# One pair of the third SwiGLU's down projection, seven products or eight

## The chip, the cores and the metric

The kernel runs on one core of a Trainium2 chip. A core has TensorE (PE in the profile; its weight loads are shown apart as PEld), VectorE (DVE), ScalarE (ACT), GpSimd (POOL) and SyncE (SP), which issues most DMA transfers. The metric is the time of one execution in device microseconds (us). The kernel before takes 942.07 us, the median of 3 runs (941.84 to 942.65).

## What is computed

A trunk of two layers over 256 tokens of width 1024, all in float32. Each layer adds half a SwiGLU, a mixer (attention), and half a SwiGLU again:

```python
def swiglu(h, w_gate, w_up, w_down):
    return (jax.nn.silu(h @ w_gate) * (h @ w_up)) @ w_down
...
    for layer in range(DEPTH):
        i = layer // 2
        h = rms_norm(x, ffn1_norm[layer])
        x = x + 0.5 * swiglu(h, ffn1_w_gate[layer], ffn1_w_up[layer], ffn1_w_down[layer])
        h = rms_norm(x, mix_norm[layer])
...
        h = rms_norm(x, ffn2_norm[layer])
        x = x + 0.5 * swiglu(h, ffn2_w_gate[layer], ffn2_w_up[layer], ffn2_w_down[layer])
    return rms_norm(x, final_norm)
```

The hidden width of a SwiGLU (D_FF) is 2816. So w_down is 2816 x 1024, or 22 blocks of 128 rows.

## The kernel before

**Stages.** There are six stages, counted from 0: SwiGLU, even mixer, SwiGLU, SwiGLU, odd mixer, SwiGLU. The third SwiGLU is stage 3; the odd mixer, stage 4, follows it. The 256 tokens are two tiles of 128 (tt 0 and 1). A stage's input is transposed on TensorE and split (`prepare`, L521), so that every matmul has it as the stationary operand, and the weights stream as the moving operand, 512 columns at a time.

**A product is three matmuls.** Float32 is reached with two parts of a value each, hi and lo. ScalarE writes hi (L479), VectorE writes lo = value - hi (L482), and a product of a left block and a piece of weights of 128 x 512 is hi x hi, hi x lo and lo x hi (`mm`, L462; the three matmuls are L471 to L473). Weights come from memory in transfers of 1 MB (`load`, L369) into one of 3 "raw" buffers, are split in two or four steps, and a raw buffer takes the next transfer when the lo of its last split is written. The split parts go into 7 buffers (hi/lo, "wp") or, where sums of weights are split, into 3 others (shi/slo, "sum").

**The order is written by hand.** Each engine works through its instructions in the order in which the program issues them. A planner decides where a weight split is issued among the products: every product is a tick (L274), a tick adds `rate` to a credit, and when the credit covers the next split and one of its buffers is free by the planner's count (`room`, L287), the hi is issued now and the lo one tick later (`supply`, L417; `low`, L438). Other work runs as small tasks that wait a written number of ticks.

**The down projection.** Its 22 row blocks are 11 pairs: pair n has blocks 2n and 2n + 1, one transfer. The list DOWN (L36) gives the order of the pairs in each stage and the form of each: `p` is a plain pair, `s` one with seven products. A plain pair takes 2 blocks x 2 token tiles x 2 halves of the 1024 columns = 8 products. A pair with seven products (`seven`, L908) takes the 2 x 2 blocks (two token tiles and two row blocks on the left, two row blocks and two column halves on the right) in Strassen's manner:

```python
            temp("1", "pj", gT[0][f + 1], b11)
...
            self.mm(Y[0][0], gT[0][f], b21, False, False)
            self.mm(Y[0][1], d4, b22, False, False)
            temp("7", "tp", d3, t7)
            temp("5", "s", d1, t5)
            self.mm(Y[1][0], gT[1][f], t8, False, False)
            temp("6", "tp", d2, t6)
```

Three go straight into the sums Y; the four called temp add up in banks of their own over all the pairs with seven products. For this the weights need four sums of 128 x 512 (t5 to t8), made on VectorE beside the splits (`strassen`, L392, L395: a "two" of 1024 columns and two steps of 512), and the left side needs four combinations of its four blocks (`quarters`, L696, and `sums_of`, L711: copies on ScalarE into the one "quarters" buffer, three steps on VectorE, then hi and lo into tiles named k and the number of the pair's first block, as k12h and k12l of pair 6). After the last pair with seven products ScalarE copies half of product 1, and `combine` (L935) adds the temps to x in eight VectorE steps spread over eight ticks. At the same place the planner's rate, 1.32 in this part (DOWN_RATE), is set to 0.34 and its credit to 3 (ENDS, L48). The last two pairs of the list are "held": their products are ordered by token tile and column half, so that each sum Y ends early, is added to x on VectorE (L614), and the next stage's transposes (L527) can begin.

**The gate and up projections of a stage** use seven products too, in two of their chunks in stage 3 (`seven_gates`, L756). The left combinations for these, four tiles called K, lie in buffers of tiles that come into use later: after two of g, in the k tiles of the two highest blocks among the pairs with seven products (the list `places` in `x_sums`, L727).

Of the kernel before, what the change touches and what calls it, by code (L numbers as in the profile page):

```python
# [35 lines left out]
DOWN = {  # L36
    0: "p0 p1 p2 s3 p4 s5 p6 s7 p8 p10 p9",
    2: "p0 p2 p1 p3 s5 p4 s7 p10 s8 p6 p9",
    3: "p0 p2 s5 s3 p4 s8 p10 s6 p1 p9 p7",
    5: "p3 p0 s2 s5 p4 s1 p9 s7 s8 p6 p10",  # L40
}

# [1525 lines left out]
```

## Time and profile before

| | |
|---|---|
| median of the runs (3) | 942.07 us (941.84 to 942.65) |
| the profiled execution | 941.97 us |
| its span, first to last instruction | 940.1 us |
| granted TensorE clock, mean | 0.998 |
| stage 3, down: first product to the next stage's first | 576.87 to 637.45 us of the span |
| DMA, mean over the span | 195 GB/s |

Times in the views are us from the span's start. A timeline row is: start, duration, engine, line, operation, written tile <- read tiles, shape, and in brackets the time for which the engine stood idle before it with what released it. Matmuls overlap, so the distance from one start to the next tells the pace. The brackets give the writer that came last, by the profile.

### The profile page before, as it was taken

Reading aid. Unit: us, or ns where it says so; the run is one execution under the profiler, and the core shown is the slowest. Engines: PE = TensorE matmul, PEld = TensorE weight load, DVE = VectorE, ACT = ScalarE, POOL = GpSimd, SP = SyncE. Lnnn points to the kernel's source line nnn. Section 1 sums busy time; section 2 is a strip of 40 time slices with the busy share of each in tenths; the row PEclk is TensorE's granted clock in tenths of the full one; section 3 lists DMA queues with packets and bytes.
Section 4 is the critical chain, followed back from the end, with each engine's and each line's share of the span. In section 5 each row is a group of like instructions: output and inputs, shape, how many; then the busy total and the mean of one; then the engine's idle time right before and its main releaser. Section 6 shows DMA issues by size and latency. Waiting matters only on the chain.

```text
span 940.1 us, 12389 instructions
## 1 busy us (share of the span) xinstructions
PE 921.0 (98%) x4399; PEld 752.3 (80%) x4399; DVE 783.1 (83%) x1212; ACT 677.5 (72%) x1091; POOL 92.6 (10%) x152
## 2 busy tenths in 40 slices
PE   9999999999999999999999999999999999999997
PEld 6887888877778787888888878778878788878886
DVE  6799778778869989888978897989767687987897
ACT  7778975477787778875657778657877577769753
POOL 1300000064410000000100000008030000000001
PEclk9999999999999999999999999999999999999999
DMA  8858875554326577767466777575534358487851
GB/s 302 286 158 250 250 235 193 181 151 108 100 91 201 203 233 230 237 211 250 153 183 223 199 235 227 204 250 172 169 102 137 132 180 245 139 254 228 218 224 45
DMA packets 129344, 183.16 MB, mean 195 GB/s; under 512 B 50689, under 2 KB 63745, under 8 KB 129281
## 3 DMA queue, kind: packets, MB, share of 16 engines
q1 hardware_dynamic: 128704, 181.58, 61.2%
q8 instruction: 34, 0.56, 0.2%
q10 hardware_dynamic: 576, 0.79, 0.2%
q14 instruction: 30, 0.24, 0.1%
HBM read 169.76 MB, written 1.05 MB: 182 GB/s over the span
## 4 chain that ended last, share of the span: by engine, by line
PE 65%; DVE 17%; ACT 10%; DMA 4%; issue 3%; POOL 0%; SPq 0%; POOLq 0%; ACTq 0%; DVEq 0%
PE pj L471 9%; PE pj L472 9%; PE pj L473 9%; PE s L472 9%; PE s L473 9%; PE s L471 9%; DVE lo L482 7%; ACT hi L479 3%; DMA glu<-turned 2%; ACT turned L560 2%; DVE raw L395 2%; PE o L1042 2%; ACT shi L479 2%; PE tp L1119 1%; PE o L472 1%
## 5 line engine op out<-in xcount | busy, mean ns | idle before, releaser
L482 DVE TENSOR_TENSOR lo<-raw,hi 128x1024 fp32r<-128x1024 f32 (+1 forms) x372 | 376.3, 1031 | 78.0 <-ACT hi L479 76.5
L479 ACT ACTIVATE hi<-raw 128x1024 fp32r<-128x1024 f32 (+1 forms) x372 | 318.6, 889 | 49.3 <-PE s L473 15.1
L471 PE MATMUL pj<-hi,th 128*128 128x512 f32 x367 | 146.7, 400 | 0.9 <-ACT glu L766 0.9
L471 PE MATMUL s<-hi,th 128*128 128x512 f32 x373 | 146.2, 392 | 0.4 <-ACT hi L479 0.4
L472 PE MATMUL pj<-lo,th 128*128 128x512 f32 x367 | 143.9, 392 | 2.6 <-DVE lo L482 2.3
L472 PE MATMUL s<-lo,th 128*128 128x512 f32 x373 | 145.5, 390 | 1.0 <-DVE lo L482 1.0
L473 PE MATMUL s<-hi,tl 128*128 128x512 f32 x373 | 145.3, 390 | 0.0
L473 PE MATMUL pj<-hi,tl 128*128 128x512 f32 x367 | 143.2, 390 | 0.0
L472 PEld LDWEIGHTS pj<-lo,th 128*128 128x128 f32 x367 | 69.0, 188 | 17.9 <-DVE lo L482 5.4
L472 PEld LDWEIGHTS s<-lo,th 128*128 128x128 f32 x373 | 70.1, 188 | 16.3 <-DVE lo L482 2.1
L471 PEld LDWEIGHTS s<-hi,th 128*128 128x128 f32 x373 | 70.0, 188 | 14.8 <-ACT hi L479 0.6
L473 PEld LDWEIGHTS s<-hi,tl 128*128 128x128 f32 x373 | 70.0, 188 | 14.6
L471 PEld LDWEIGHTS pj<-hi,th 128*128 128x128 f32 x367 | 69.0, 188 | 15.4 <-ACT glu L766 1.3
L473 PEld LDWEIGHTS pj<-hi,tl 128*128 128x128 f32 x367 | 68.9, 188 | 14.6
L491 POOL TENSOR_TENSOR rstd<-var,mhalf 128x1 f32<-128x1 f32 (+2 forms) x16 | 17.1, 1069 | 593.7 <-ACT th L512 314.7
L560 ACT COPY turned<-glu 128x1024 uint16<-128x1024 uint16 (+1 forms) x48 | 60.1, 1253 | 9.7 <-DMA glu<-turned 9.7
L479 ACT ACTIVATE shi<-raw 128x1024 fp32r<-128x1024 f32 x30 | 31.7, 1058 | 42.9 <-DVE raw L395 26.1
L556 ACT COPY turned<-glu 128x1024 uint16<-128x1024 uint16 (+1 forms) x48 | 46.4, 966 | 21.7 <-DVE glu L794 15.7
L471 PE MATMUL s<-hi,g_h 128*128 128x512 f32 (+1 forms) x131 | 51.3, 392 | 0.0
L473 PE MATMUL s<-hi,g_l 128*128 128x512 f32 (+1 forms) x131 | 50.8, 388 | 0.0
L472 PE MATMUL s<-lo,g_h 128*128 128x512 f32 (+1 forms) x131 | 50.8, 388 | 0.0
L482 DVE TENSOR_TENSOR slo<-raw,shi 128x1024 fp32r<-128x1024 f32 x30 | 36.7, 1223 | 10.8 <-ACT shi L479 10.4
(482 smaller groups left out, 1671.1 us busy)
## 6 DMA issues: line engine op xcount, KB each, us to landing
raw<-in_ffn_w_down SPq DMA_DIRECT2D x44, 1024.0 KB, 5.1
raw<-in_ffn_w_up SPq DMA_DIRECT2D x28, 1024.0 KB, 5.3
raw<-in_ffn_w_gate SPq DMA_DIRECT2D x26, 1024.0 KB, 5.2
raw<-in_ffn_w_gate SPq DMA_DIRECT2D x35, 512.0 KB, 4.1
raw<-in_ffn_w_up SPq DMA_DIRECT2D x32, 512.0 KB, 5.0
raw<-in_odd_w_qkv SPq DMA_DIRECT2D x12, 1024.0 KB, 5.1
raw<-in_even_w_in SPq DMA_DIRECT2D x4, 1024.0 KB, 5.2
raw<-in_even_w_out SPq DMA_DIRECT2D x8, 512.0 KB, 5.8
```

Source lines behind the costliest of these rows:

```text
L395: add = lambda o, x, y: self.nc.vector.tensor_tensor(o, x, y, op=ALU.add)
L471: mm(ps, h, wh, start=first, stop=False)
L472: mm(ps, h, wl, start=False, stop=False)
L473: mm(ps, l, wh, start=False, stop=last)
L479: self.nc.scalar.activation(hi, src, AF.Copy)
L482: self.nc.vector.tensor_tensor(lo, src, hi.bitcast(F32), op=ALU.subtract)
L491: nc.gpsimd.tensor_tensor(r[:, :n], v[:, :n], self.mhalf[:, :n], op=ALU.pow)
L556: self.nc.scalar.copy(planes.rearrange("p (h c) -> p h c", h=2), back.rearrange("p (c h) -> p h c", h=2))
L560: self.nc.scalar.copy(planes.rearrange("p (c h) -> p h c", h=2), back.rearrange("p (h c) -> p h c", h=2))
L1042: self.nc.tensor.matmul(O[64 * s : 64 * s + 64, i * P : i * P + P], v(b0 + i, s, kc), pT[s][:, i, kc, :], start=(kc == 0), stop=(kc == 1),)
L1119: nc.tensor.transpose(tb[:, o : o + P], p[:, i, kc * P : kc * P + P], self.ident)
```

## The change

The letter of one pair in the list of stage 3: pair 6, eighth of eleven, becomes plain.

```diff
 DOWN = {
     0: "p0 p1 p2 s3 p4 s5 p6 s7 p8 p10 p9",
     2: "p0 p2 p1 p3 s5 p4 s7 p10 s8 p6 p9",
-    3: "p0 p2 s5 s3 p4 s8 p10 s6 p1 p9 p7",
+    3: "p0 p2 s5 s3 p4 s8 p10 p6 p1 p9 p7",
     5: "p3 p0 s2 s5 p4 s1 p9 s7 s8 p6 p10",
 }
```

Pair 6 then takes eight products where it took seven. Its sums of weights (L395) and the combinations of blocks 12 and 13 (L701 to L715, k12h and k12l) are not made; its weights are split as two splits of two pieces, in wp buffers. Pairs 5, 3 and 8 keep the seven products. The last of them is now pair 8, sixth in the list, so the half copy of product 1, `combine` and the setting of the planner to ENDS follow pair 8 instead of pair 6, two pairs earlier:

```python
        order = [i for i, (kind, _) in enumerate(down) if kind == "strassen"]
        for i, (kind, pair) in enumerate(down[:-HELD]):
            if kind == "strassen":
                seven(pair, i == order[0], i == order[-1])
                if i == order[-1]:
                    self.start(combine())
                    self.rate, self.due = ENDS[self.now.n]
                continue
```

The two highest blocks among the pairs with seven products are 16 and 10 where they were 16 and 12, so the fourth of the K tiles lies in k10h and k10l where it lay in k12h and k12l.

## The prediction

> **What bounds the kernel now.** I read the busy totals first, then the windows over the stage that changes, then TensorE's timeline in it, and last the chain of waits behind each gap.
>
> ```profile
> PE 921.0 (98%) x4399; PEld 752.3 (80%) x4399; DVE 783.1 (83%) x1212; ACT 677.5 (72%) x1091; POOL 92.6 (10%) x152
> ```
>
> ```profile
> 576.87:589.11 12.24, 12.24 (x55) 10.14 (x54) 9.98 (x13) 9.85 (x15) 0.00 (x0) 1.00 0.55 142
> 589.11:598.05 8.94, 8.52 (x37) 6.60 (x36) 8.87 (x14) 7.14 (x12) 0.00 (x0) 1.00 0.36 122
> 598.05:608.25 10.20, 10.20 (x46) 8.45 (x45) 10.16 (x12) 6.42 (x7) 0.00 (x0) 1.00 0.65 235
> 608.25:618.45 10.20, 10.20 (x46) 8.45 (x45) 10.09 (x11) 5.92 (x6) 0.00 (x0) 1.00 0.69 261
> 618.45:630.70 12.25, 12.25 (x55) 9.95 (x53) 10.77 (x16) 5.83 (x9) 0.00 (x0) 1.00 0.78 276
> 630.70:637.45 6.75, 5.23 (x27) 4.27 (x27) 5.23 (x13) 4.36 (x14) 0.20 (x1) 1.00 0.42 150
> ```
>
> A window's row gives its length, then the busy time of PE, PEld, DVE, ACT and POOL, the granted clock (1.00 throughout) and DMA. The third SwiGLU's down projection is 576.87 to 637.45. TensorE is busy in all but two windows; in the second and the last it loses time. VectorE is full from 589 to 618 (8.87 of 8.94, 10.16 of 10.20, 10.09 of 10.20). So TensorE sets the end, and here VectorE sets TensorE's two gaps:
>
> ```profile
> 576.87 0.39 PE L471 MATMUL o<-hi,g_h 128*128 128x512 f32 x1
> ...
> 596.79 0.50 PE L472 MATMUL s<-slo,g_h 128*128 128x512 f32 x1 [0.42 <-DVE slo L482]
> ...
> 598.05 0.39 PE L471 MATMUL o<-hi,g_h 128*128 128x512 f32 x1
> ...
> 630.47 0.39 PE L473 MATMUL s<-hi,g_l 128*128 128x512 f32 x1
> 632.37 0.66 PE L527 MATMUL tp<-mats,x 128*128 128x128 f32 x4 [1.52 <-DVE x L614]
> ...
> 637.45 0.40 PE L471 MATMUL pj<-hi,th 128*128 128x512 f32 x1
> ```
>
> The price of a matmul is its distance to the next, not its 0.39 us. From 598.05 to 630.47 lie 143 steps (48 products of three, less one): 32.42 / 143 = 0.2267 us. A product is 0.680 us.
> From 576.87 to 598.05 lie 30 products, 20.40 us at that pace, and they took 21.18: **0.78 us** lost in the first gap (0.42 shown idle, the rest slower starts round it). At the end the transposes could start at 630.47 + 0.23 = 630.70 and start at 632.37: **1.67 us** lost in the second.
>
> **The change part by part.** (1) TensorE. Pair 6 takes four piece rows by two token tiles: 8 products where the seven-product form takes 7. One product more, 3 x 0.2267 = **+0.68 us**, on the bounding engine, hidden by nothing.
>
> (2) VectorE, in the down stage. What goes is in these rows, start to start:
>
> ```profile
> 605.73 2.96 DVE L482 TENSOR_TENSOR lo<-raw,hi 128x1024 fp32r<-128x1024 f32 x3
> 608.60 1.22 DVE L395 TENSOR_TENSOR two<-raw 128x1024 f32<-128x1024 f32 x1
> 609.74 1.22 DVE L482 TENSOR_TENSOR lo<-raw,hi 128x1024 fp32r<-128x1024 f32 x1
> 610.87 0.69 DVE L395 TENSOR_TENSOR raw<-two,raw 128x512 f32<-128x512 f32 x1
> 611.59 0.69 DVE L395 TENSOR_TENSOR raw<-raw 128x512 f32<-128x512 f32 x1
> 612.20 1.22 DVE L482 TENSOR_TENSOR slo<-two,shi 128x1024 fp32r<-128x1024 f32 x1
> 613.49 1.23 DVE L482 TENSOR_TENSOR slo<-raw,shi 128x1024 fp32r<-128x1024 f32 x1
> 614.63 4.63 DVE L482 TENSOR_TENSOR lo<-raw,hi 128x1024 fp32r<-128x1024 f32 x4
> ```
>
> The last of the three at 605.73 (2.87 less two full lows of 1.14, 0.6) and all until 614.63 is pair 6: 0.6 + 6.0 = 6.6 us. A plain pair is two lows, 2.3 us. VectorE sheds 4.3 us, ScalarE the matching highs. The load is the same 1,024 KB at the same place of SP's queue.
>
> (3) The left factors of pair 6 (blocks 12 and 13) lose their combinations:
>
> ```profile
> 574.55 0.28 DVE L714 TENSOR_TENSOR quarters<-quarters 128x128 f32<-128x128 f32 x1
> 574.87 0.29 DVE L715 TENSOR_TENSOR quarters<-quarters 128x128 f32<-128x128 f32 x1
> ...
> 581.50 0.68 DVE L482 TENSOR_TENSOR k12l<-quarters,k12h 128x512 fp32r<-128x512 f32 x1
> 583.62 0.48 DVE L677 SCALAR_TENSOR_TENSOR glu<-s,rstd,silu 128x256 f32<-128x256 f32 x1 [1.43 <-ACT silu L672]
> ```
>
> ```profile
> 576.55 1.05 ACT L479 ACTIVATE hi<-raw 128x1024 fp32r<-128x1024 f32 x1
> 577.50 0.62 ACT L479 ACTIVATE k12h<-quarters 128x512 fp32r<-128x512 f32 x1
> ...
> 582.28 0.42 ACT L701 ACTIVATE quarters<-turned 128x256 f32<-128x256 f32 x1 [2.39 <-DVE k12l L482]
> ```
>
> VectorE sheds about 1.2 us here (0.3 and 0.3, and 0.6 of k12l), ScalarE k12h. More than that: there is one "quarters" buffer, and pair 8's ScalarE copy waits 2.39 us for k12l to release pair 6's; behind it stand the silu for which VectorE idles 1.43 us, and the highs of the first sums. Nothing of pair 6 is left to wait for. I walked both queues from 574 with the rows' durations: VectorE's two lows of pair 5's sums end at 584.1, the last low of pair 3's sums, for which TensorE waits at 596.79, at about 593.6 instead of 596.7. TensorE wants it at product 28, 595.9. So the **0.78 us** of the first gap go, with 2.3 us in hand. What is late next there is that low itself: its buffer is released by pair 5's third and fourth products (about 591.4), so it can hardly come sooner.
>
> (4) The last seven-product pair is now pair 8. ScalarE's half copy of product one, the eight combining steps and the switch to ENDS (0.34 per product, credit 3) move two pairs forward, past p10 and the old pair 6.
>
> ```profile
> raw<-in_ffn_w_down SPq DMA_DIRECT2D x44, 1024.0 KB, 5.1
> ```
>
> ```profile
> 614.75 0.37 SPq L379 DMA_DIRECT2D raw<-in_ffn_w_down  x1
> ```
>
> ```profile
> 619.58 2.01 ACT L479 ACTIVATE hi<-raw 128x1024 fp32r<-128x1024 f32 x2 [2.33 <-DMA raw<-in_ffn_w_down]
> ```
>
> ```profile
> 620.67 3.58 DVE L482 TENSOR_TENSOR lo<-raw,hi 128x1024 fp32r<-128x1024 f32 x4 [1.41 <-ACT hi L479]
> 624.17 0.68 DVE L941 SCALAR_TENSOR_TENSOR x<-pj,x 128x512 f32<-128x512 f32 x1
> ...
> 630.42 1.29 DVE L482 TENSOR_TENSOR lo<-raw,hi 128x512 fp32r<-128x512 f32 x2
> 631.63 0.69 DVE L614 SCALAR_TENSOR_TENSOR x<-o,x 128x512 f32<-128x512 f32 x1
> ```
>
> Before, the add to x that the next stage's transposes wait for (631.63) stands in VectorE's queue behind the combining steps and odd lows (624.17 to 631.63), four lows before them, and a 1.41 us wait for highs that wait 2.33 us for pair 7's load: that one was issued at 614.75, when the second sums' low of the old pair 6 released its buffer. Now that buffer is released by p6's second low, at about 607. I counted the planner's credits product by product (call the first of down 0). Pair 8's sevens end after product 44. Highs then come only as a released buffer allows: pair 9's second at product 49, pair 7's at 53 and 57, the first odd pieces at 61, 62, 65, 67, 70 and 73. All of pair 6, pair 1 and half of pair 9 are made before that. With releases at TensorE's pace and loads landing 5.1 us after issue, VectorE is through with combining near 618, with pair 7's second low near 620.4 (TensorE wants it at product 72, 576.87 + 72 x 0.680 = 625.8), and free for the add to x when its sum ends, about 627.0 to 627.7. The transposes stand before product 79, at 630.6. So the **1.67 us** go too, 3 us in hand. TensorE then waits for nothing in this stage. Of the moved steps the copy stands behind pair 1's highs on ScalarE, which wait for pair 1's load; combining follows it, and behind combining stand the lows of pairs 9 and 7, the ones with 5 us in hand. None issues a DMA; SP's queue keeps its order with pair 7 and the first odd loads issued some 6 us earlier, and POOL has no work in these windows (0.00) to be moved past.
>
> (5) What follows. Entering the odd stage the count gives the same credit (0.02), the same five live buffers and the same order as before, one product later. So that stage is not rearranged, only moved. Its loads are issued earlier, not later.
>
> (6) The K[3] factors of the gate stages take the buffer of block 10 (pair 5) instead of block 12 (pair 6), which block 10's own factors overwrite later:
>
> ```profile
> L472 PE MATMUL tp<-slo,k12h x4: 389/389/389, 492.2 to 539.1; 128*128 128x512 f32 x4
> ```
>
> ```profile
> 552.63 0.61 ACT L479 ACTIVATE k10h<-quarters 128x512 fp32r<-128x512 f32 x1
> ```
>
> The last read is at 539.1, the overwrite at 552.63: a new wait with 13 us in hand, nothing. Were that cover gone, ScalarE would stand there, with the highs behind it. The buffers that block 12 no longer needs let the pool's last tiles sit 4 KB lower; over those the odd stage lays its attention outputs, which it makes last, so that costs nothing either.
>
> **Sum.** +0.68 - 0.78 - 1.67 = -1.77 us. The profiled execution took 941.97 us for a span of 940.1; it would take 940.20, span 938.3. The median of the runs is 0.10 above it: 942.07 - 1.77 = **940.3 us**, 0.19% less. About 0.2%, 1.9 us, is what a measurement of this kernel tells from no change, so the likeliest verdict is "within 0.2%", close to the edge.
>
> **A rule that speaks against it.** TensorE is at 98% busy and VectorE at 83%. The Trainium skill, "Perfetto Trace Analysis", section "Identifying the Most-Contended Engine", says to take the engine of highest occupancy for the bottleneck and to optimize that one first; by it this change loads the wrong engine, and the sum would be the +0.68 of step 1 instead of -1.77. The same page of the Trainium skill, section "Optimization Strategy", adds that the most contended engine can change between regimes; the windows above agree (VectorE 10.16 of 10.20 us), and that is why I do not follow the whole-span rule here.
>
> **The rivals.** *Only the product counts.* Both gaps stay: another wait on ScalarE (a transposed tile's DMA) takes the place of the quarters buffer, combining takes the place of pair 6: 942.07 + 0.68 = 942.75. Against it stand the 5.5 us that VectorE sheds; for it, that VectorE stays nearly full until 611. This is the case of the Trainium skill's rule above. *The first gap stays*, the second goes: 942.07 + 0.68 - 1.67 = 941.1. For it: the chain through DMA transposes and one quarters buffer is long, and I have walked it with medians. *The second stays*, the first goes: 942.07 + 0.68 - 0.78 = 942.0. For it: odd lows still stand ahead of the add to x.
> *Slower: starved at the held pairs.* Credit 0.34 now rules 40 products instead of 24, and the held pairs use four splits within four products (69 to 72). Pairs 9 and 7 are made one by one behind releases; a late one costs a high (0.95, from 576.55 to 577.50) and a low (1.14) in a row, 2.1 us. With two late: 940.3 + 4.2 = 944.5. It decides where pair 7's second low comes after 625.8; I have it at 620.4, so VectorE would have to be 5.4 us behind my walk. That the change does not do what it says cannot be: the counts are fixed.
>
> **How the numbers follow.** Both gaps go: 0.70 (its own range 939.8 to 940.8). The first stays: 0.09. The second stays: 0.07. Only the product counts: 0.06. Starved: 0.08. The range for 8 in 10 takes in the first three: 939.7 to 942.0. Faster begins below 940.19, 0.11 under the forecast: a bit under half of the first case lies there, 0.32. Slower, above 943.95, holds the starved case but for a mild one, 0.07. The rest, 0.61, is within.
>
> **What would show it.** Right: no PE idle by slo between 594 and 598, no ACT wait for k-low before L701 near 580, transposes of the next stage right behind their matmul, combining near 612 to 618, and the odd stage's first matmul at 635.7. Wrong: a PE wait at the held pairs; the odd stage gaining PE waits of its own, which would return what was won; a first odd matmul later than 637.

## The result and the profile after

The changed kernel takes **940.45 us** (median of 19 runs, 940.16 to 941.56), the kernel before, measured beside it, 941.98 us (19 runs). The ratio over all the runs is **0.9982**, 95% interval 0.9976 to 0.9988; of the two medians it is 0.9984. The forecast was 940.3 us and "within 0.2%". The profiled execution took 940.38 us for a span of 938.5.

The busy totals of the changed kernel:

```profile
PE 921.4 (98%) x4402; PEld 753.3 (80%) x4402; DVE 777.6 (83%) x1203; ACT 675.8 (72%) x1086; POOL 92.7 (10%) x152
```

TensorE has three matmuls more and the same share of the span; the totals don't show what happened. The windows over the stage do (columns as before: length, busy time of PE, PEld, DVE, ACT and POOL with counts, granted clock, DMA share, GB/s; cut at places that answer to those of before):

```profile
576.72:588.96 12.24, 12.24 (x56) 10.14 (x55) 11.29 (x16) 11.40 (x18) 0.00 (x0) 1.00 0.76 220
588.96:597.90 8.94, 8.94 (x41) 7.42 (x40) 8.91 (x11) 5.50 (x8) 0.00 (x0) 1.00 0.36 110
597.90:608.10 10.20, 10.20 (x47) 8.45 (x46) 9.69 (x11) 6.19 (x7) 0.00 (x0) 1.00 0.68 256
608.10:618.30 10.20, 10.20 (x47) 8.45 (x46) 9.04 (x12) 6.35 (x7) 0.00 (x0) 1.00 0.72 273
618.30:630.55 12.25, 12.25 (x57) 10.10 (x55) 8.01 (x12) 3.46 (x6) 0.00 (x0) 1.00 0.75 258
630.55:635.48 4.93, 4.93 (x27) 4.11 (x26) 3.03 (x9) 4.37 (x14) 0.22 (x1) 1.00 0.00 2
sum 58.76, PE 58.76 PEld 48.66 DVE 49.97 ACT 37.28 POOL 0.22; mean PE 9.79 PEld 8.11 DVE 8.33 ACT 6.21 POOL 0.04
```

TensorE is busy for the whole of every window: both gaps are gone. VectorE and ScalarE do in the first window what they could not do before (11.29 of 12.24 us where it was 9.98; 11.40 where it was 9.85): the wait for the quarters buffer is not there. From 608 on VectorE has room, which it did not have before (9.04 of 10.20 against 10.09).

The stage, from its first product to the next stage's first, takes 635.48 - 576.72 = **58.76 us**, where it took 637.45 - 576.87 = 60.58: **-1.82 us**, with -1.77 forecast. From here on this stage time is the measure: it depends least on what lies elsewhere in the execution.

ScalarE's timeline, where the 2.39 us wait stood:

```profile
578.14 1.38 ACT L560 COPY turned<-glu 128x1024 uint16<-128x1024 uint16 x1 [0.81 <-DMA glu<-turned]
579.55 0.42 ACT L701 ACTIVATE quarters<-turned 128x256 f32<-128x256 f32 x1
```

The copy into quarters waits for nothing. What ends last there now is the transposing DMA ahead of it, 0.81 us. VectorE's timeline at the places that the prediction named:

```profile
583.02 1.22 DVE L482 TENSOR_TENSOR slo<-raw,shi 128x1024 fp32r<-128x1024 f32 x1
...
592.79 1.22 DVE L482 TENSOR_TENSOR slo<-raw,shi 128x1024 fp32r<-128x1024 f32 x1
...
612.70 0.68 DVE L941 SCALAR_TENSOR_TENSOR x<-pj,x 128x512 f32<-128x512 f32 x1
...
617.68 1.28 DVE L939 TENSOR_TENSOR x<-x,glu 128x512 f32<-128x512 f32 x2
618.88 4.76 DVE L482 TENSOR_TENSOR lo<-raw,hi 128x1024 fp32r<-128x1024 f32 x6
...
626.55 0.69 DVE L614 SCALAR_TENSOR_TENSOR x<-o,x 128x512 f32<-128x512 f32 x1 [0.76 <-PE o L473]
629.27 0.69 DVE L614 SCALAR_TENSOR_TENSOR x<-pj,x 128x512 f32<-128x512 f32 x1 [2.03 <-PE pj L473]
```

The low for which TensorE had waited ends at about 594.0 (592.79 + 1.22) where it ended near 596.7. Combining runs from 612.70 to 618.96. The adds to x now wait for TensorE's sums, 0.76 and 2.03 us; before, TensorE waited 1.52 us for one of them. TensorE's timeline has no bracket from 576.72 to the odd stage:

```profile
595.75 0.39 PE L471 MATMUL s<-shi,g_h 128*128 128x512 f32 x1
595.98 0.39 PE L472 MATMUL s<-slo,g_h 128*128 128x512 f32 x1
...
630.21 0.39 PE L473 MATMUL s<-hi,g_l 128*128 128x512 f32 x1
630.44 0.60 PE L527 MATMUL tp<-mats,x 128*128 128x128 f32 x4
...
635.48 0.39 PE L471 MATMUL pj<-hi,th 128*128 128x512 f32 x1
```

The matmul at 595.98 is the one that stood behind the first gap. It starts 0.23 us after the matmul before it, where that step took 0.81 us (595.98 to 596.79 before). Up to the transposes one matmul follows the next at 0.227 us, and the transposes start 0.23 us behind the matmul before them.

### The profile page after: what moved, and what is told of

Its sections match the earlier page's. It is cut to its first block, busy times and chain, and to the rows that moved or that the text cites. A ratio compares the mean times of both kernels' runs of the same rounds, so it can differ in the third digit from the quotient of the medians.

```text
span 938.5 us, 12381 instructions
## 1 busy us (share of the span) xinstructions
PE 921.4 (98%) x4402; PEld 753.3 (80%) x4402; DVE 777.6 (83%) x1203; ACT 675.8 (72%) x1086; POOL 92.7 (10%) x152
## 4 chain that ended last, share of the span: by engine, by line
PE 76%; DVE 11%; ACT 8%; issue 3%; DMA 2%; POOL 0%; SPq 0%; POOLq 0%; ACTq 0%; DVEq 0%
PE s L472 10%; PE s L473 10%; PE s L471 10%; PE pj L471 10%; PE pj L472 10%; PE pj L473 10%; DVE lo L482 5%; ACT hi L479 3%; PE o L473 2%; PE o L472 2%; PE o L471 2%; PE o L1042 2%; ACT turned L560 2%; DMA glu<-turned 1%; PE tp L1119 1%
```

## The experiments

The result agrees with the steps, but several things changed at once: the quarters buffer, VectorE's work, the place of combining. Each was changed alone. (A "seven" is a pair with seven products; a "gap" is one of TensorE's two, behind product 28 and ahead of the transposes.) In what follows "stage" is the time from the first product of stage 3's down projection to the odd stage's first; 60.58 us before, 58.76 after. In one repetition of the changed kernel, `after_again`, it was 58.77, so it repeats to some hundredths. Each stage time is of one profiled execution. "Measured" gives the ratio to the kernel before with its 95% interval of about 0.0009 to each side, 0.9 us; so the ratios do not tell most of these kernels apart.

**1. The quarters wait alone.** The kernel before, all four sevens kept; block 12's high is issued four ticks sooner, and its low stands one tick closer behind it, so five ticks sooner in all:

```diff
-            yield SUMS_WAIT[0]
+            early = self.now.n == 3 and f == 12
+            yield 4 if early else SUMS_WAIT[0]
...
-            yield SUMS_WAIT[1]
+            yield 1 if early else SUMS_WAIT[1]
```

> Four pairs keep the seven products, as before; only the hi and lo of pair 6's left combinations are issued five products sooner, so that the quarters buffer is free for pair 8. Stage time is from the first down product to the odd stage's first (60.58 us before, 58.76 after the change). Theory, the first gap is the wait for the quarters buffer and the second is VectorE's lag carried on: the gap at product 28 closes (0.78 us), VectorE runs some 2 us ahead from there and the second gap closes wholly or mostly: stage 58.1 to 58.9 us, 939.5 to 940.4 us in all, with no product added. Rival, the amount of work that pair 6 puts on VectorE makes both gaps: stage 60.3 to 60.6 us, about 942. Between them, only the first gap closes: 59.8 us, 941.2.

Measured: ratio 0.9986 (0.9977 to 0.9996), stage **58.90 us**. ScalarE's row in this kernel, and TensorE's one row with a wait:

```profile
580.56 0.42 ACT L701 ACTIVATE quarters<-turned 128x256 f32<-128x256 f32 x1
```

```profile
631.39 0.44 PE L527 MATMUL tp<-mats,x 128*128 128x128 f32 x2 [0.61 <-DVE x L614]
```

The wait at L701 is gone and with it the whole first gap; of the second 0.77 us are left (0.61 shown idle). So these two waits (the numbers behind the two `yield`s) are worth 60.58 - 58.90 = 1.68 us in the stage without a product more. The work of VectorE and ScalarE is the same as before; only its order differs. The quarters buffer was behind the first gap and behind more than half of the second. In the whole less of it arrived: the medians are 942.52 and 941.73 us, 0.79 apart. Run 9 shows where 0.9 us went.

**2. Combining late.** The changed kernel with the combining and the switch to ENDS put back behind pair 6:

```diff
-                if i == order[-1]:
-                    self.start(combine())
-                    self.rate, self.due = ENDS[self.now.n]
+                if i == order[-1] and self.now.n != 3:
+                    close()
...
+            if self.now.n == 3 and pair == 6:
+                close()
```

> The changed kernel with combining and the switch of the planner's rate put back behind pair 6, where they were before. Theory, the second gap closed because VectorE sheds work and a raw buffer is released sooner, not because combining moved: stage 58.8 us, 940.4 us in all, the transposes not waiting. Rival, it closed because combining moved two pairs forward: the wait of the transposes for the add to x returns, up to 1.67 us, stage up to 60.4 us, 942.1.

Measured: 0.9983 (0.9974 to 0.9992), stage **58.75 us**, no gap. Where combining stands made no difference here: VectorE's add to x ends at 629.18 us, and TensorE comes to the transposes at 631.93, 2.75 us later.

**3. The combinations of blocks 12 and 13 kept**, though nothing reads them:

```diff
+        if self.now.n == 3:
+            paired[12] = []
```

> The changed kernel, but the left combinations of pair 6 are still made (and not used), so the quarters buffer is held for them as before and the K tiles lie where they lay. Theory, the quarters buffer alone makes the first gap: ScalarE's wait of about 2.4 us for k12's lo returns, and with it a wait of TensorE at product 28 of 0.4 us idle, 0.7 to 0.8 us with the slower starts; the second gap stays closed: stage 59.5 us, 941.2 us in all. Rival, the first gap closed because VectorE has less of anything queued: stage 58.8, 940.4.

Measured: 0.9983 (0.9974 to 0.9992), stage **59.64 us**. ScalarE's row, and TensorE's:

```profile
582.98 0.42 ACT L703 ACTIVATE quarters<-turned 128x256 f32<-128x256 f32 x1 [2.40 <-DVE k12l L482]
```

```profile
597.47 0.50 PE L472 MATMUL s<-slo,g_h 128*128 128x512 f32 x1 [0.42 <-DVE slo L482]
```

The wait is back with 2.40 us, and the first gap with the 0.42 us idle of before (0.87 in all, where it was 0.78: the steps round it are a little slower). The second stays closed: by then VectorE has made up the delay. Together with run 1 this settles the first gap.

**4. Two sevens.** The changed kernel with pair 8 plain too, the last two K tiles in k16 and k12 as in the kernel before, and the switch to ENDS left behind pair 8 (those lines are not shown); combining moves up behind pair 3:

```diff
-    3: "p0 p2 s5 s3 p4 s8 p10 p6 p1 p9 p7",
+    3: "p0 p2 s5 s3 p4 p8 p10 p6 p1 p9 p7",
...
+            tops = [16, 12] if self.now.n == 3 else sorted(paired, reverse=True)
```

> The changed kernel with pair 8 plain as well (two pairs with seven products are left; the planner's rate is still switched behind pair 8). No gap is left to close, so this prices one product by itself. Theory: plus 0.68 us, stage 59.44 us, 941.1 us in all. Rival, relieving VectorE goes on paying: 940.4 or less. If combining still earlier or pair 8's two wp splits collide with the buffers, a wait shows in the stage and it is over 941.5.

Measured: 0.9982 (0.9973 to 0.9991), stage **59.42 us**, no gap: 0.66 more than with three sevens. That is the price of a product, 0.68 by the prediction. With no gap left to close, relieving VectorE once more returns nothing.

**5. VectorE's work put back.** The changed kernel; behind the two lows of pair 6 stand four sums of 128x1024 on a spare tile, which nothing reads:

```diff
+        def spare():
+            for view in views:
+                two = self.t([P, 2, 512], "two")
+                self.nc.vector.tensor_tensor(two, view, view, op=ALU.add)
+
+        return [Split(view, [2], view is views[-1], then=spare) for view in views]
```

> The changed kernel with four VectorE sums of 128x1024 (1.14 us each, 4.6 us in all) on a spare tile put back at pair 6's place, behind its two lows; they are not used. So VectorE has the work that the change took away, TensorE keeps its extra product, and combining stays two pairs forward. Theory (the gaps went by the quarters buffer and by combining early; VectorE had 8.8 us idle in the stage after the change): still no gap, stage 58.8 us, within 0.2. Rival (the gaps went because VectorE has less to do): the second gap is back, stage 60 to 60.4.

Measured: 0.9981 (0.9972 to 0.9990), stage **58.76 us**. The stage in one window:

```profile
578.56:637.32 58.76, 58.76 (x264) 48.64 (x263) 54.30 (x71) 37.18 (x58) 0.22 (x1) 1.00 0.63 208
```

VectorE is busy for 54.30 us of it, nearly the 55.10 of before, and TensorE waits for nothing. The sums stand behind the place of the first gap, so this tests the second. VectorE's first add to x in this kernel:

```profile
629.32 0.68 DVE L626 SCALAR_TENSOR_TENSOR x<-o,x 128x512 f32<-128x512 f32 x1
```

It ends at 630.00, and TensorE comes to the transposes at 632.28, 2.28 us later. So it was not the 4.3 us of pair 6 that VectorE sheds. With run 2: once the quarters wait is gone, either early combining or the lighter pair is enough for the second gap, and both together are more than it needs. With neither (run 1) 0.77 us of it stay. One thing differs between run 1 and these two besides: the product more, by which TensorE comes to the transposes 0.68 us later and which by itself would have hidden nearly all of the 0.77. It isn't what closed the gap in runs 2 and 5, where 2.75 and 2.28 us are in hand, more than three times its size.

**6. Starved at the held pairs.** The changed kernel with less credit behind the last seven:

```diff
-ENDS = {0: [0.43, 0], 2: [0.4, 1], 3: [0.34, 3], 5: [0.26, 2]}
+ENDS = {0: [0.43, 0], 2: [0.4, 1], 3: [0.2, 0], 5: [0.26, 2]}
```

> The changed kernel with ENDS of stage 3 at 0.2 and 0 instead of 0.34 and 3: by the count of credits pair 9's second split is made at product 56 (49), pair 7's at 66 and 72 (53 and 57), where TensorE takes that last one at product 72. Rival of the prediction (starved at the held pairs): a high and a low made at the moment they are wanted cost 2.1 us in a row, so TensorE waits about 2 us at product 72 and the stage goes from 58.8 to 60.9 us. Other theory: a place in the order is no time; ScalarE and VectorE run ahead of TensorE through their queues, and with the same buffers and loads the pieces are there when wanted: stage 58.8 to 59.1, and what comes late is the odd stage's first pieces, whose lows now stand behind the adds to x: at most 1.5 us of waits in its first 10 us.

Measured: 962.62 us, 1.0217 (1.0203 to 1.0232); stage **58.76 us**, no wait at product 72, and **some 20 us lost behind the stage**. TensorE's waits from 635 us on (what waited for what: us in total, times, longest):

```profile
PE pj L472 <- DVE lo L482: 9.0, 10, 2.5
PE pj L471 <- ACT hi L479: 3.0, 5, 1.0
PE s L472 <- DVE lo L482: 1.4, 2, 0.8
```

These add up to 13.4 us, of which the changed kernel has 1.3. The rest of the loss is slower steps round the waits and a lower granted clock: 0.83 from 670 to 680 us and 0.87 from 715 to 725, where the changed kernel has 1.00 from 640 to 760. The clock's share is at most some 3 us, an estimate from these two windows (0.17 and 0.13 of 10 us each).

The rival named the wrong place and far too low a price. A piece that stands late in the order is no late piece as long as ScalarE and VectorE run ahead of TensorE; in the down stage they do (VectorE stood idle for 4.67 us before its first add to x). In the odd stage a piece of weights serves two products, so the planner must make 0.5 a product, and its rates there are 0.39 to 0.51. A deficit with which it enters is not made up, and pieces go on being issued just when they are wanted. The other expectation had this place, but at most 1.5 us in the first 10; there it was about 4 us, and it went on to 20.8 at TensorE's last matmul.

**7. A wait far behind the change.** The change's lead did not last to the end: TensorE has a wait in the last SwiGLU that it did not have before. TensorE's rows of the changed kernel, and of the kernel before at the same products:

```profile
821.29 0.39 PE L471 MATMUL pj<-hi,th 128*128 128x512 f32 x1
822.04 0.50 PE L472 MATMUL pj<-lo,th 128*128 128x512 f32 x1 [0.36 <-DVE lo L482]
```

```profile
823.27 0.39 PE L471 MATMUL pj<-hi,th 128*128 128x512 f32 x1
823.75 0.50 PE L472 MATMUL pj<-lo,th 128*128 128x512 f32 x1
```

The step takes 0.75 us where it took 0.48: 0.27 us given back. The low is late because one of ScalarE's highs is, and that high, in the changed kernel, starts 1.07 us after the start of VectorE's sum ahead of it (814.74 against 813.67), where it was 0.79 before (816.45 against 815.66):

```profile
813.67 0.69 DVE L395 TENSOR_TENSOR raw<-raw 128x512 f32<-128x512 f32 x1
```

```profile
814.74 1.06 ACT L479 ACTIVATE shi<-raw 128x1024 fp32r<-128x1024 f32 x1 [1.19 <-PE pj L473]
```

The instructions and their waits are the same in both from there to the end; ScalarE's program up to there is five instructions shorter. Hence a kernel with five one-column copies more:

```diff
                 nc.scalar.activation(M["c"], M["1"], AF.Copy, scale=0.5)
+                for _ in range(5 if self.now.n == 3 else 0):
+                    nc.scalar.activation(M["c"][:, :1], M["c"][:, :1], AF.Copy)
```

> The changed kernel with five more ScalarE copies of one column onto itself behind the half copy of product one in stage 3, so that ScalarE's program has 949 instructions behind that point as before the change, not 944. In two kernels with 944 a high of the last SwiGLU starts 1.07 us after VectorE's sum before it (0.79 in those with 949, 947 and 939), and TensorE waits 0.36 us for its low. Theory (the wait hangs on where the program stands in ScalarE's instruction stream): 0.79 again, no such wait, TensorE's lead of the stage kept to the end, span 0.26 us shorter than after the change with the same start of the stage. Rival (it comes of TensorE's lead itself): 1.07 stays and the wait too. The down stage itself 58.8 us by both.

Measured: 940.94 us, 0.9979 (0.9970 to 0.9988), stage 58.76. VectorE's sum and ScalarE's high behind it in this kernel:

```profile
814.50 0.69 DVE L395 TENSOR_TENSOR raw<-raw 128x512 f32<-128x512 f32 x1
```

```profile
815.28 1.06 ACT L479 ACTIVATE shi<-raw 128x1024 fp32r<-128x1024 f32 x1 [0.91 <-DVE raw L395]
```

815.28 - 814.50 = 0.78 us, and TensorE does not wait at that low (822.10 to 822.57, 0.47 us). The theory said so, and `sums_back` and `combine_late`, whose ScalarE programs have the length of the changed kernel's, have the wait. That it hangs on the place in ScalarE's program is shown. What delays the high, the trace does not say outright: it names a product of TensorE as the releaser, but that is inferred. It does show DMA packets of a queue that carries instructions. In the four profiles with the late high (the changed kernel twice and those two) such a packet starts 0.65 to 0.90 us behind the high's start, at 815.39 in the changed kernel; with the five copies it starts at 810.24, 5 us ahead of it. In `two_sevens` and `starved_ends` one starts 1.0 to 1.1 us behind the high, and the high is not late. This fits the loading of ScalarE's instructions as the cause and does not prove it. The ratios can't tell 0.27 us apart; the rows do.

**8. The second gap without the lighter pair.** Run 1's kernel with ENDS of stage 3 at 0.3 and 0, which issues the lows of the odd stage's first pieces ("odd lows") later. One of them now stands behind the first add to x, not two as the expectation has it; others move back behind later steps:

```diff
-ENDS = {0: [0.43, 0], 2: [0.4, 1], 3: [0.34, 3], 5: [0.26, 2]}
+ENDS = {0: [0.43, 0], 2: [0.4, 1], 3: [0.3, 0], 5: [0.26, 2]}
```

> The kernel before with its four sevens, block 12's high and low taken five products sooner, and ENDS of stage 3 at 0.3 and 0 instead of 0.34 and 3, so that two odd lows of 0.6 us that stood ahead of the add to x stand behind it. Theory (the quarters wait made the first gap, the work ahead of the add to x the second, and no product need be added): no gap, 254 matmuls, stage 78 products and 0.4 us of transposes, 58.1 us (58.90 with the sooner high alone, less 0.77; the kernel before 60.58, after the change 58.76); ratio about 0.9975. Rival (the second gap hangs on the late load of pair 7 and the combining behind pair 6, not on the two lows): the add to x comes no sooner, stage 58.9. Either way the odd pieces made later may cost a wait in the first 10 us of the odd stage.

Measured: stage **58.17 us**, the gaps closed but for 0.07 us ahead of the transposes, and yet the ratio is 0.9997 (0.9988 to 1.0007). (The stage has 84 products; the 78 of the expectation are those ahead of the transposes.) TensorE's waits from 635 us on:

```profile
PE pj L472 <- DVE lo L482: 0.9, 1, 0.9
PE s L473 <- DVE tl L517: 0.6, 1, 0.6
PE s L472 <- DVE lo L482: 0.6, 1, 0.6
```

The first of these is in the kernel before too. The other two, at 755.46 and 759.26, are new: TensorE's lead over run 1 goes from 1.12 us at 696 to a lag of 0.65 at 761. The stage's gain was given back 120 us later.

**9. The same with the planner's credit restored** on entering the odd stage, beside the changed kernel once more:

```diff
         rates = iter(ODD_RATE)
+        self.due += 0.12
```

> As k12_lean_end (four sevens, block 12's high and low sooner, ENDS of stage 3 at 0.3 and 0), with 0.12 added to the planner's credit on entering the odd stage, which makes every later order that of the kernel before again; only three lows near the add to x stand elsewhere. Theory (the stage's 58.17 us are worth their 2.4 us, and k12_lean_end lost 1.75 us near 755 to 760 only by the credit that it carried into the next stages): stage 58.2, no wait for tl or lo at 755 to 760, total 2.2 to 2.4 us under the kernel before, ratio 0.9975, 0.5 us under the changed kernel. Rival (the later waits come of the lead itself): waits near 755 again, ratio 0.999 to 1.000.

> The changed kernel once more, beside k12_lean_even on one chip. Stage 58.76 us, the wait of 0.36 us at the last SwiGLU's low again, ratio 0.9982, whatever the first product of the stage stands at (it stood at 576.7 to 578.6 us in the profiles so far, by what the first 10 us of the kernel took).

Measured: k12_lean_even 940.34 us, 0.9983 (0.9974 to 0.9992), stage **58.06 us**; after_again 940.43 us, 0.9984 (0.9975 to 0.9993), stage 58.77. With the credit the waits near 755 don't come, and from 2 us into the odd stage on ScalarE and VectorE do everything in the order of the kernel before: the loss of run 8 was the planner's. But of the 2.4 us expected only 1.6 arrived. TensorE was 2.37 us ahead at its last matmul, and so was the issue of the last store (934.04 against 936.41), while the span was 1.5 shorter. From that issue to the end of the span it took 4.6 us, against 3.7. (The expectations of run 10 count from the end of the issuing instruction, 0.4 us later.) The DMA view over that stretch of k12_lean_even (queue: packets, MB, share; then the stores and their time to landing):

```profile
q10 hardware_dynamic: 144, 0.26, 15.3%
q1 hardware_dynamic: 144, 0.26, 15.3%
q14 instruction: 1, 0.01, 0.4%
...
out<-shi ACTq DMA_DIRECT2D x1, 256.0 KB, 3.6
```

One packet of the instruction queue stands among the packets of the last store. It does in k12_sooner, k12_lean_end and k12_lean_even, and in none of the other kernels profiled up to there; in those the store ends 0.9 us sooner after its issue.

**10. Whose packet it is.** k12_lean_even with the five one-column ScalarE copies of run 7, or with five one-column VectorE multiplications by one in the gate part, so that what follows stands five instructions later in that engine's program:

> k12_lean_even with the five one-column ScalarE copies of five_more_act behind stage 3's half copy. In the three kernels with block 12's high taken sooner the last store takes 4.3 us from its issue to the end, 3.3 to 3.4 in the others, and in those three alone a packet of the instruction queue falls into it; so k12_lean_even has TensorE 2.38 us ahead at its end and 1.4 of it in the span. Theory (the packet stands where an engine's program says, and that engine is ScalarE): it leaves the store, which takes 3.4 us again, and the ratio goes from 0.9983 to about 0.9974. If it is another engine's packet: 4.3 us and 0.9983 as before. Stage 58.1 either way.

```diff
+            for _ in range(5 if (self.now.n, f0, tt) == (3, 0, 0) else 0):
+                nc.vector.tensor_scalar(m[:, :1], m[:, :1], 1.0, 0.0, op0=ALU.mult, op1=ALU.add)
```

> k12_lean_even with five one-column VectorE multiplications by one (on the first glu tile of stage 3, some 0.1 us each, where VectorE has room) instead of ScalarE's copies. Theory (the packet in the last store belongs to VectorE's program): the store takes 3.4 us from its issue to the end, ratio about 0.9974. If it is another engine's packet: 4.3 us and 0.9983. Stage 58.1 either way.

Measured: with VectorE's five, **940.21 us, ratio 0.9970** (0.9960 to 0.9980), stage 58.09, the last store 3.7 us from issue to end; with ScalarE's five, 941.64 us, 0.9987 (0.9978 to 0.9996), the store 4.7 us. The DMA view over the last stretch of the kernel with VectorE's five:

```profile
q1 hardware_dynamic: 144, 0.26, 18.9%
q10 hardware_dynamic: 144, 0.26, 18.8%
...
out<-shi ACTq DMA_DIRECT2D x1, 256.0 KB, 2.6
```

The packet has left the store: it starts at 930.41 us, 3.7 us ahead of the store's issue, where in k12_lean_even it started 1.9 us behind the issue. It is moved by VectorE's program and not by ScalarE's. That the packet itself holds up the store is inferred from the two always coming together (four kernels with both, all the others with neither). This kernel, with all four sevens, has the lowest ratio of the study, 0.9970 against 0.9982 for the change. The intervals of the two overlap (0.9960 to 0.9980 and 0.9976 to 0.9988), and it ran on another chip than the repetition of the change; so that it is the fastest is likely and not settled by the ratios. In the profiles it takes 360.8 us from the stage's first product to the end of the span, the change 361.8 and the kernel before 363.3.

One thing went wrong with ScalarE's five: the stage was to be 58.1 and was 59.05. Its rows, ScalarE's and then VectorE's:

```profile
620.67 1.15 ACT L930 ACTIVATE silu<-silu 128x1 f32<-128x1 f32 x5
621.73 2.18 ACT L479 ACTIVATE hi<-raw 128x512 fp32r<-128x512 f32 x4
```

```profile
630.44 0.69 DVE L614 SCALAR_TENSOR_TENSOR x<-o,x 128x512 f32<-128x512 f32 x1
```

The five copies take 1.15 us just ahead of highs for which VectorE waits, and with four sevens VectorE has nothing in hand there: the add to x comes 1.3 us later than in k12_lean_even, where it stood at 629.10 (1.2 us later if counted from the stage's start), and TensorE waits 0.79 us for it.

## Why the prediction was right

By its steps:

1. **The product more**, +0.68 us: 0.66 in run 4.
2. **VectorE sheds 4.3 us.** It does (55.10 us busy in the stage before, 49.97 after; the difference of 5.13 is pair 6's 4.3, k12l's 0.6 and some 0.2 that was not traced). The 1.2 us that step 3 adds for the combinations leaves out one VectorE step of block 12, 0.34 us at 573.61 (L707), so that VectorE sheds some 5.9 us in all and not 5.5. But run 5 shows that this was not needed for the gain. The prediction used it as one of three reasons and did not weigh them; a reader could take from it that a lighter VectorE pays, and run 4 shows that it doesn't.
3. **The quarters wait and the first gap.** Right in mechanism, place and size: 0.78 us, shown from both sides by runs 1 and 3. The walk through the two queues was off by little: 584.1 for the end of pair 5's sums (measured 584.2), 593.6 for that of pair 3's (594.0, of which TensorE has need at 595.98: 2.0 us in hand where 2.3 were forecast).
4. **The second gap.** Right in size (1.67 us gone), combining near 618 (618.96), transposes at 630.6 (630.44), first odd product at 635.7 (635.48). Its account was incomplete. It gave the gap to the combining steps and the earlier load; run 1 shows that 0.90 of the 1.67 us came of the quarters wait too, by what it held up behind it, and runs 2 and 5 that for the other 0.77 the lighter pair or the early combining is each enough. The prediction books the product as a cost alone; it also brings TensorE to the transposes 0.68 us later, which hides that much of the gap. It was not needed: the first add to x ends at 627.24, 3.2 us before TensorE comes to the transposes, so the "3 us in hand" is right. Pair 7's second low ended at 621.2, 0.8 us later than forecast.
5. **The odd stage only moved.** Right: no wait of its own. What the step left out lies later still: 0.27 us were given back in the last SwiGLU (run 7).
6. **K[3] in k10.** Nothing, as forecast: ScalarE's k10h has no wait.

The sum for the stage was -1.77 us and the stage gave -1.82. In the profiled execution 0.27 of it went in the last SwiGLU and 0.15 came from an earlier start of the stage, which leaves 1.7 us at TensorE's last matmul (933.58 to 931.87) and 1.6 in the span (940.1 to 938.5); the medians differ by 1.53 us. The earlier start is well within what such starts vary by (last section); that it makes up for half of the loss in the last SwiGLU is luck.

The rule of the most contended engine, weighed in the prediction, was rightly not followed: TensorE was at 98% and got more to do, and the kernel became faster. But the reason that was given (VectorE is full in these windows) was only half of it. What decided was one buffer, on which ScalarE waited 2.39 us with VectorE's work standing behind it. Run 5 has VectorE nearly as full as before, and TensorE waits for nothing.

Two readings of the prediction need setting right here. The window that it quotes for VectorE (10.16 of 10.20 us) has TensorE busy for all of its 10.20; the one in which VectorE has more than TensorE is 589.11 to 598.05 (8.87 against 8.52 of 8.94). And the rule is told without its exception: the same section of the Trainium skill, "Perfetto Trace Analysis", "Identifying the Most-Contended Engine", judges TensorE's headroom by the busy share of its weight loads and by its share of peak flops, not by how long its matmuls are busy. Here the weight loads are busy for 80% of the span and VectorE for 83%, so the rule does not clearly name TensorE.

Of the rivals, the three that kept a gap did not come, and the starved one had a wrong mechanism (run 6). A real one on the slower side was there and was not named: a planner that enters the next stage with less credit.

## What to carry to other kernels

Look in a gap for the first wait upstream that is no engine's own work, here one buffer's release, and try to move just that: two shorter waits in the program gave 1.68 us in the stage, where the change gave 1.82 by another road and at the price of a product. Two causes may each be enough for one gap; only taking them back one at a time shows which are needed, and the time that is left in hand shows by how much. When a planner carries a credit from stage to stage, restore it where an edit ends, or compare the orders behind it: 0.12 of a credit was worth 1.75 us, a hundred microseconds later.

## What the hardware showed that was not expected

- **A packet of the instruction queue can go with lost time.** Where one stands among the packets of the last store, the store takes 0.9 us more (4.6 to 4.7 us from issue to the end, against 3.7 to 3.8). Five VectorE instructions of one column, which change no value, moved it away, and the time from the stage's first product to the end of the span went from 361.7 to 360.8 us. (The ratios, 0.9983 and 0.9970, are of two chips, and their intervals overlap.)
- **A place in ScalarE's program** cost 0.27 us in one step, in the kernels with one length of program and not in those with others (1.06 us from VectorE's sum to ScalarE's high in four profiles, 0.78 to 0.79 in the rest).
- **Programs that are the same up to the stage enter it at different times**: the first down product stood at 576.72 to 578.56 us in these profiles. Between the changed kernel and `sums_back` 0.8 us of this were there after 10 us and 1.04 after 71. So single spans differ by as much as the change is worth, while the time of the stage repeats: 58.75 to 58.77 us in the six profiles whose stage has the changed kernel's products and no gap.
